# A two-layer flow block on one core: the low half of the grouped-query keys stored on 128 rows instead of 64

## The chip, the cores and the metric

The kernel runs on one core of a Trainium2 chip. It is one launch: inputs come from device memory, the result goes back to device memory, and what is measured is the device time of that launch in microseconds (us). Five engines work side by side, each through its own list of instructions: TensorE (PE, with its weight loads shown apart as PEld), VectorE (DVE), ScalarE (ACT), GpSimd (POOL), and SyncE (SP), which issues the transfers. Times are the median of three runs. One further execution was profiled, and it gives the rows below.

## The reference, cut to what matters

The model has two layers over 512 latent tokens and 256 context tokens, width 1024. Each layer mixes tokens in four groups (a convolution, a latent attention "MLA", a grouped-query attention "GQA", a retention) and ends in a feed-forward block. The change touches the scores of GQA alone: four query heads of width 64 share two key heads, and all 768 keys are seen by the latent queries.

```python
def grouped_attention(q, k, v):          # q: [b, kv, group, lq, 64]
    scale = dq ** -0.5
    def one_block(qblk):
        s = jnp.einsum('bkgqd,bksd->bkgqs', qblk, k) * scale
        p = jax.nn.softmax(s, axis=-1)
        return jnp.einsum('bkgqs,bksd->bkgqd', p, v)

yc_l = merge_heads(grouped_attention(gqa_q(q_l, gqa_q_g, pos),
                                     jnp.concatenate([gk_c, gk_l], axis=2),
                                     jnp.concatenate([gv_c, gv_l], axis=2)))
...
x = x + g1 * y_lat
x = x + g2 * sq_relu_mlp(modulate(x, sh2, sc2), mlp_w1[layer], mlp_w2[layer])
```

In layer 0 the context tokens are queries as well (over the 256 context keys); in layer 1 only the latents are.

## The kernel before, in words

**Numbers.** TensorE is fed with tiles of type F32R. So that little is lost, an fp32 operand x is kept as two such tiles, a high half (x copied to F32R) and a low half (x minus the high half). `split` writes both: a copy, then a subtraction. A product of two such operands is the sum of high times low, high times high and low times high, all summed in PSUM.

**GQA scores.** A head has width 64, half of TensorE's 128 rows. `gqa_prep` puts that to use. For each key head it transposes the keys into PSUM (64 rows by 512 latent or 256 context keys) and writes three things: `kd`, the high half, twice, on rows 0 to 63 and again on rows 64 to 127 (lines 1399 and 1400); and `kl`, the low half, on rows 0 to 63 (line 1401). For each unit (a query head and a pair of token tiles) it writes `qd`: the high half of the queries on rows 0 to 63, the low half on rows 64 to 127. The scores are then two passes (line 1089): pass 0 takes 64 rows of `qd` as stationary and `kl` as moving operand, which is high times low; pass 1 takes all 128 rows of `qd` and `kd`, which is high times high plus low times high. Each pass is one weight load and one matmul for 512 keys and one for 256 keys.

**Units.** A unit has two query tiles. For each there are the passes into one PSUM tile of 768 scores, a minimum over them on DVE, an exponential with its sum on ACT, a reciprocal on DVE, and a scaling on DVE, ACT or POOL (`scores`). `finish`, which is recorded after the next unit's scores, transposes the probabilities on TensorE, splits them, and multiplies them with the values. In layer 0 GQA has 12 units (4 heads by 3 pairs of tiles), of which the 4 on context tokens see only 256 keys; in layer 1 it has 8. So pass 0 is run 8·2·2 + 4·2·1 = 40 times in layer 0 and 8·2·2 = 32 times in layer 1, 72 times in all.

**Order.** The program is recorded first and then scheduled by a planner in the same file (`Plan`, lines 112 to 645), which holds an own cost for every instruction, walks a clock, and gives each engine its list of instructions. The list is fixed when the kernel runs. The planner's cost of a matmul goes by its columns and not by its rows. Some copies may go to DVE, ACT or POOL; the planner picks. All instructions are issued from line 645, so the profile's rows bear that line, and SBUF pages are all named `m`, PSUM banks `b` (one bank) or `pp` (two-bank tiles or halves of them), small columns `ty`.

Of the kernel before, what the change touches and what calls it, by code (L numbers as in the profile page):

```python
# [9 lines left out]
F32 = mybir.dt.float32  # L10
F32R = mybir.dt.float32r
AF = mybir.ActivationFunctionType
ALU = mybir.AluOpType
# [686 lines left out]
def block_kernel(ctx: ExitStack, tc: tile.TileContext, x, c, cx, c_ctx, w_mod, b_mod, w_in, w_out,  # L700
# [11 lines left out]
    V, S, G, T, D = plan.V, plan.S, plan.G, plan.T, plan.D  # L712
# [13 lines left out]
    def smt(shape, dt=F32, nm="sm"):  # L726
        return plan.tile(ph, "sm", shape, dt, nm)
# [13 lines left out]
    def psT(shape=(128, 512), nm="psT"):  # L741
        return plan.tile(ph, "t", shape, F32, nm, gang=True)
# [265 lines left out]
    def mixing(l, ht, yt, todo, late=None):  # L1008
# [9 lines left out]
        p = psT()  # L1018
# [8 lines left out]
        p = psT()  # L1027
# [38 lines left out]
        def tile_of(d, t):  # L1066
            for pr in PAIRS:
                if t in pr:
                    return d[pr][:, pr.index(t)]
# [317 lines left out]
        def gqa_prep(h, pr, whole):  # L1387
            def f():
                kv = h // 2
                if kv not in kgs:  # L1390
                    kds = {}
                    for a, ts in ((0, LAT), (512, CTX)):
                        p = psT()
                        n = 128 * len(ts)
                        kd, kl = kds[a] = [a3t([128, n], F32R, nm="kd") for _ in range(2)]
                        for i, t in enumerate(ts):
                            T.transpose(p[0:64, i * 128:(i + 1) * 128], tile_of(ug, t)[:, 256 + kv * 64:320 + kv * 64],
                                        ident)
                        VS.copy(out=kd[0:64], in_=p[0:64, 0:n])
                        VS.copy(out=kd[64:128], in_=p[0:64, 0:n])  # L1400
                        V.tensor_tensor(out=kl[0:64], in0=p[0:64, 0:n], in1=kd[0:64].bitcast(F32), op=ALU.subtract)
                    kgs[kv] = kds
                kds = kgs[kv]
                qd = smt([128, 256], F32R, nm="qd")
                p = psT()
                for i in range(2):
                    T.transpose(p[0:64, i * 128:(i + 1) * 128], ug[pr][:, i, h * 64:h * 64 + 64], ident)
                VS.copy(out=qd[0:64], in_=p[0:64, 0:256])
                V.tensor_tensor(out=qd[64:128], in0=p[0:64, 0:256], in1=qd[0:64].bitcast(F32), op=ALU.subtract)
                return (lambda i, n: qd[0:(64, 128)[n], i * 128:(i + 1) * 128],  # L1410
                        lambda n, a: kds[a][1][0:64] if n == 0 else kds[a][0],
                        (lambda t: tile_of(ug, t)[:, 384 + kv * 64:448 + kv * 64]) if whole else
                        (lambda t: tile_of(vg, t)[:, kv].rearrange("p a d -> p (a d)")))
            return f
# [487 lines left out]
```

## Time and profile before

| | |
|---|---|
| median of 3 runs | 1861.64 us (1861.56 to 1864.9) |
| the profiled execution | 1851.87 us |
| its span, first to last instruction | 1850.2 us |
| mean granted TensorE clock | 0.971 of full speed |
| PE busy | 1713.0 us, 93% of the span |
| DVE busy | 1356.5 us, 73% |
| ACT, POOL busy | 678.8 us (37%), 386.4 us (21%) |
| read from device memory | 161.14 MB, 88 GB/s over the span |

The first row of the table is what a change is measured by, the second is the execution that the trace shows. "Busy" is a share over the whole span, and the stages differ: the feed-forward blocks are long runs of matmuls, while in the two stretches with GQA scores (about 334 to 472 us in layer 0 and 1334 to 1426 us in layer 1) TensorE, DVE and ACT hand work to each other. The rows on those stretches stand further below. In the rows, `64*128` is a stationary operand of 64 rows and 128 columns, and the next figure, as 64x512, the moving operand.

### The profile page before, as it was taken

To read this page: it belongs to the slowest core of one execution; us is meant where nothing else is said; L and a number is where in the kernel's file an instruction comes from. 1 tells how busy PE (TensorE), PEld (TensorE's weight loads), DVE (VectorE), ACT (ScalarE), POOL (GpSimd) and SP (SyncE) were. 2 spreads that over 40 slices of the span, in tenths; PEclk is the share of its full clock that TensorE was granted. 3 is DMA by queue.
4 is the path that set the end of the run, shared out by engine and by line. 5 is a ranking of instruction groups with operands and counts; after the bars stand their busy time and mean duration, and the time that the engine had idled before them with its cause. 6 is when DMAs were issued, how large, how long until landed. Compare 5 with 4: busy or idle time off the path is not lost. (4 is left out here: it accounts for less than half of the span.)

```text
span 1850.2 us, 23212 instructions
## 1 busy us (share of the span) xinstructions
PE 1713.0 (93%) x8587; PEld 1393.5 (75%) x8587; DVE 1356.5 (73%) x2305; ACT 678.8 (37%) x1256; POOL 386.4 (21%) x355
## 2 busy tenths in 40 slices
PE   6995789989999999999999999959898989999998
PEld 4784668655788888888888889758766778888886
DVE  5889348877897788777775677974988776666665
ACT  5522028866434112112112126213987331122122
POOL 3328013541401000100100022120434521100001
PEclk9997899989999999999999999969999999999999
DMA  9220022443232334334331212110122523333331
GB/s 303 67 75 12 19 79 80 139 118 115 79 112 72 103 114 144 108 113 148 124 93 58 68 48 84 44 52 12 32 61 74 166 81 102 105 100 92 102 92 57
DMA packets 140641, 168.67 MB, mean 91 GB/s; under 512 B 7658, under 2 KB 93274, under 8 KB 140528
## 3 DMA queue, kind: packets, MB, share of 16 engines
q1 hardware_dynamic: 140528, 167.20, 29.4%
q8 instruction: 67, 1.10, 0.2%
q14 instruction: 46, 0.38, 0.1%
HBM read 161.14 MB, written 2.10 MB: 88 GB/s over the span
## 5 line engine op out<-in xcount | busy, mean ns | idle before, releaser
L645 PE MATMUL b<-m,m 128*128 128x512 f32 (+6 forms) x6400 | 1347.8, 368 | 43.3 <-DVE m L645 32.3
L645 PEld LDWEIGHTS b<-m,m 128*128 128x128 f32 (+2 forms) x6400 | 1107.2, 189 | 257.0 <-DVE m L645 30.4
L645 DVE TENSOR_TENSOR m<-m,m 128x1024 fp32r<-128x1024 f32 (+10 forms) x669 | 549.5, 840 | 135.0 <-PE b L645 81.2
L645 ACT CAST m<-m 128x1024 fp32r<-128x1024 f32 (+5 forms) x354 | 277.3, 804 | 661.5 <-PE b L645 470.0
L645 POOL TENSOR_TENSOR m<-m,m 128x1024 fp32r<-128x1024 f32 (+11 forms) x155 | 261.0, 1693 | 1106.2 <-ACT m L645 613.4
L645 DVE TENSOR_TENSOR m<-b,m 128x512 f32<-128x512 f32 (+12 forms) x337 | 203.7, 614 | 121.5 <-PE b L645 105.4
L645 PE MATMUL pp<-m,m 128*128 128x512 f32 (+9 forms) x904 | 227.1, 371 | 22.1 <-ACT m L645 10.9
L645 PEld LDWEIGHTS pp<-m,m 128*128 128x128 f32 (+3 forms) x904 | 153.0, 190 | 76.4 <-issue 24.2
L645 PE MATMUL b<-ident,m 128*128 128x128 f32 (+4 forms) x744 | 114.3, 279 | 32.3 <-DVE m L645 29.4
L645 ACT COPY m<-b 128x512 f32<-128x512 f32 (+6 forms) x177 | 82.0, 483 | 128.3 <-PE b L645 123.5
L645 PEld LDWEIGHTS b<-ident,m 128*128 128x128 f32 (+4 forms) x744 | 86.3, 141 | 53.9 <-DVE m L645 34.3
L645 DVE TENSOR_TENSOR m<-m 128x512 f32<-128x512 f32 (+2 forms) x107 | 67.4, 631 | 77.1 <-ACT m L645 76.4
L645 DVE CAST m<-m 128x512 fp32r<-128x512 f32 (+6 forms) x163 | 76.9, 474 | 57.6 <-DMA m<-in_w_mod_dram 31.3
L645 DVE SCALAR_TENSOR_TENSOR m<-m,sf,m 128x1024 f32<-128x1024 f32 x80 | 103.6, 1307 | 19.6 <-DMA m<-in_w_mod_dram 19.6
L645 ACT ACTIVATE m<-b 128x512 f32<-128x512 f32 (+1 forms) x117 | 61.8, 531 | 152.6 <-PE b L645 150.1
L645 DVE SCALAR_TENSOR_TENSOR m<-m,cvw,m 128x783 f32<-128x783 f32 (+1 forms) x120 | 100.8, 890 | 0.6
L645 DVE TENSOR_REDUCE ty<-pp 128x1 f32<-128x768 f32 (+1 forms) x67 | 61.9, 929 | 20.0 <-PE pp L645 19.5
L645 ACT ACTIVATE m<-pp,ty 128x768 f32<-128x768 f32 (+1 forms) x67 | 59.1, 883 | 14.2 <-DVE ty L645 6.1
L645 ACT ACTIVATE m<-m 128x1024 f32<-128x1024 f32 (+4 forms) x65 | 42.0, 649 | 51.3 <-DVE m L645 41.6
L645 POOL TENSOR_TENSOR ty<-ty,mhalf 128x1 f32<-128x1 f32 (+4 forms) x47 | 58.6, 1253 | 2.0
L645 DVE TENSOR_SCALAR m<-m,ty 128x512 f32<-128x512 f32 (+3 forms) x98 | 49.7, 542 | 8.8 <-POOL ty L645 8.1
L645 ACT CAST m<-b 128x512 fp32r<-128x512 f32 (+6 forms) x84 | 41.2, 500 | 38.6 <-PE b L645 37.6
(113 smaller groups left out, 629.5 us busy)
## 6 DMA issues: line engine op xcount, KB each, us to landing
m<-in_mlp_w_dram SPq DMA_DIRECT2D x128, 512.0 KB
m<-in_w_mod_dram SPq DMA_DIRECT2D x96, 512.0 KB
m<-in_w_in_dram SPq DMA_DIRECT2D x32, 512.0 KB
m<-in_w_out_dram SPq DMA_DIRECT2D x16, 512.0 KB
m<-in_x_dram SPq DMA_DIRECT2D x8, 512.0 KB
m<-in_dist_dram SPq DMA_DIRECT2D x16, 256.0 KB
m<-in_w_in_dram SPq DMA_DIRECT2D x8, 416.0 KB
m<-m SPq DMA_DIRECT2D x24, 96.0 KB
```

The costliest lines, as they stand in the source:

```text
L645: op.fn(*[f(a) for a in op.args], **{k: f(a) for k, a in op.kw.items()})
```

## The change

The low half of the keys is written a second time, to rows 64 to 127 of `kl`, by one more subtraction on DVE for each key head and each of the two key ranges: 8 instructions in all. Pass 0 then takes the whole of `qd` (128 rows) as its stationary operand and the whole of `kl` as the moving one. It so computes high times low plus low times low. The number of matmuls and weight loads stays what it was.

```diff
                         V.tensor_tensor(out=kl[0:64], in0=p[0:64, 0:n], in1=kd[0:64].bitcast(F32), op=ALU.subtract)
+                        V.tensor_tensor(out=kl[64:128], in0=p[0:64, 0:n], in1=kd[0:64].bitcast(F32), op=ALU.subtract)
                     kgs[kv] = kds
...
-                return (lambda i, n: qd[0:(64, 128)[n], i * 128:(i + 1) * 128],
-                        lambda n, a: kds[a][1][0:64] if n == 0 else kds[a][0],
+                return (lambda i, n: qd[:, i * 128:(i + 1) * 128],
+                        lambda n, a: kds[a][1 - n],
                         (lambda t: tile_of(ug, t)[:, 384 + kv * 64:448 + kv * 64]) if whole else
```

Since the planner sees eight more instructions, it gives other lists for the mixing stages of both layers. In the feed-forward blocks the rows stay the same but for the names of pages, apart from a few rows that follow a mixing stage.

On DVE, at the second key head of layer 0, the low half for the latent keys (tile `m_6987`, out of PSUM tile `pp_6699`) was one subtraction of 64x512 behind the two copies of the high half:

```order
L645 TENSOR_TENSOR m_6034<-b_3587,m_6034 64x256
L645 CAST m_5011<-pp_6699 64x512 x2
L645 TENSOR_TENSOR m_6987<-pp_6699,m_5011 64x512
L645 CAST m_6941<-b_3585 64x256 x2
L645 TENSOR_SCALAR kdt_914<-kdt_914 128x16
```

With the change, the same place has the tile under the name `m_7017`, from `pp_6957`, with the first of the two copies of the high half four rows further up:

```order
L645 CAST m_6034<-pp_6957 64x512
L645 TENSOR_REDUCE ty_3568<-pp_6981 128x1
L645 TENSOR_TENSOR m_3638<-b_3587,m_3638 64x256
L645 TENSOR_TENSOR m_6924<-pp_6956,m_6924 64x256
L645 CAST m_6034<-pp_6957 64x512
L645 TENSOR_TENSOR m_7017<-pp_6957,m_6034 64x512
L645 RECIPROCAL ty_3569<-ty_3575 128x1
L645 TENSOR_TENSOR m_7017<-pp_6957,m_6034 64x512
L645 TENSOR_REDUCE ty_3565<-pp_7025 128x1
```

The second subtraction has come in behind a reciprocal and ahead of the minimum (the reduction) of a unit, and other work of DVE now stands between the copies.

On PE, the first latent unit's scores (into `pp_6579`, from the page `m_6283` with the low half, `m_3841` with the high half, `m_5961` and `m_6034` for the context keys) stood as one block of four:

```order
L645 MATMUL b_3585<-m_6538,m_4425 128x256 x4
L645 MATMUL pp_6579<-m_6283,m_5961 128x512
L645 MATMUL pp_6579<-m_3841,m_5961 128x512
L645 MATMUL pp_6579<-m_5961 128x256
L645 MATMUL pp_6579<-m_6034,m_5961 128x256
L645 MATMUL b_3587<-m_6476,sc 2x512
```

Now (into `pp_6561`, the queries and the low half both in `m_6283`) they stand among the matmuls of an MLA unit's values, into `pp_6546`:

```order
L645 MATMUL b_3586<-m_6437,sc 4x512
L645 MATMUL pp_6561<-m_6283 128x512
L645 MATMUL pp_6546<-m_6527,m_4516 128x256 x3
L645 MATMUL pp_6546<-m_6531,m_4584 128x256
L645 MATMUL pp_6561<-m_3841,m_6283 128x512
L645 MATMUL pp_6546<-m_6531,m_4584 128x256 x3
L645 MATMUL pp_6561<-m_6283 128x256
L645 MATMUL pp_6561<-m_6034,m_6283 128x256
L645 MATMUL pp_6546<-m_6569,m_4425 128x256
```

The same four matmuls are there, and other matmuls have moved in between the two passes.

## Rows read from the trace of the kernel before

**Rows 1.** The page: busy time of each engine over the span (share, instructions).

```profile
PE 1713.0 (93%) x8587; PEld 1393.5 (75%) x8587; DVE 1356.5 (73%) x2305; ACT 678.8 (37%) x1256; POOL 386.4 (21%) x355
```

**Rows 2.** Windows: busy us (x instructions) per engine, granted clock, DMA; seven stretches.

```profile
core 0: us, PE busy (x) PEld busy (x) DVE busy (x) ACT busy (x) POOL busy (x), PEclk, DMA share, GB/s
290.00:334.00 44.00, 41.48 (x289) 34.50 (x288) 42.09 (x94) 39.77 (x85) 22.33 (x18) 1.00 0.31 94
334.00:472.00 138.00, 129.56 (x611) 79.24 (x609) 107.59 (x218) 99.36 (x217) 52.19 (x50) 0.94 0.41 125
1290.00:1334.00 44.00, 39.10 (x255) 32.17 (x253) 42.44 (x95) 42.48 (x90) 13.79 (x12) 1.00 0.09 29
1334.00:1426.00 92.00, 83.41 (x408) 54.88 (x406) 76.47 (x159) 74.72 (x157) 35.49 (x40) 1.00 0.19 56
362.00:369.00 7.00, 7.00 (x22) 4.28 (x22) 4.68 (x6) 4.01 (x7) 2.61 (x2) 0.51 0.46 145
386.00:396.00 10.00, 7.23 (x23) 5.29 (x24) 7.41 (x18) 4.29 (x10) 2.33 (x4) 0.50 0.40 101
1201.00:1232.00 31.00, 11.24 (x35) 8.97 (x36) 29.64 (x103) 5.06 (x7) 12.05 (x16) 0.51 0.09 26
```

**Rows 3.** Timeline of PE, 348.6 to 353.2: start us, us, tiles, form, count.

```profile
348.37 0.40 PE L645 MATMUL b<-m,m 128*128 128x256 f32 x2
348.70 0.92 PE L645 MATMUL pp<-m,m 64*128 64x512 f32 x2
...
351.78 0.92 PE L645 MATMUL pp<-m,m 64*128 64x512 f32 x2
352.63 0.38 PE L645 MATMUL pp<-m 64*128 64x256 f32 x1
352.94 0.38 PE L645 MATMUL pp<-m,m 128*128 128x256 f32 x1
353.17 0.40 PE L645 MATMUL b<-m,sc 128*4 128x512 f32 x1
```

**Rows 4.** Timeline of PEld in the same stretch: each weight load.

```profile
351.77 0.18 PEld L645 LDWEIGHTS pp<-m,m 64*128 64x128 f32 x1 [0.47 <-issue]
352.20 0.19 PEld L645 LDWEIGHTS pp<-m,m 128*128 128x128 f32 x1 [0.24 <-issue]
352.63 0.18 PEld L645 LDWEIGHTS pp<-m 64*128 64x128 f32 x1 [0.24 <-issue]
```

**Rows 5.** Timeline of PE in both feed-forward blocks: 128x512, 128x256 back to back.

```profile
1599.65 8.60 PE L645 MATMUL b<-m,m 128*128 128x512 f32 x37
...
842.82 2.79 PE L645 MATMUL b<-m,m 128*128 128x256 f32 x22
```

**Rows 6.** Groups of PE by form: 64-row stationaries (two of five).

```profile
L645 PE MATMUL pp<-m,m 64*128 64x512 f32 x26 | 13.1, 505 | 2.6 <-DVE m L645 1.6 <-ACT m L645 0.8
L645 PE MATMUL pp<-m,m 64*128 64x256 f32 x33 | 13.0, 393 | 0.0
```

**Rows 7.** Waits of DVE, 334:472 and 1334:1426: us, times, longest us.

```profile
DVE ty L645 <- PE pp L645: 9.6, 12, 2.4
...
DVE ty L645 <- PE pp L645: 7.7, 7, 1.9
```

**Rows 8.** Timeline of DVE, then PE, at the second key head of layer 0.

```profile
385.63 0.68 DVE L645 TENSOR_TENSOR m<-pp,m 64x512 fp32r<-64x512 f32 x1
...
386.46 2.00 PE L645 MATMUL pp<-m,m 64*128 64x512 f32 x3 [1.61 <-DVE m L645]
```

**Rows 9.** Groups of DVE by form: 64-row subtractions out of PSUM.

```profile
L645 DVE TENSOR_TENSOR m<-b,m 64x256 fp32r<-64x256 f32 x14 | 5.8, 417 | 0.4
...
L645 DVE TENSOR_TENSOR m<-b,m 64x512 fp32r<-64x512 f32 x3 | 2.0, 671 | 0.0
```

**Rows 10.** Timeline of PE, from 1219 us, ahead of a fall of the clock.

```profile
1219.06 1.11 PE L645 MATMUL pp<-ident,m 128*128 128x128 f32 x4 [5.45 <-ACT m L645]
1228.10 18.13 PE L645 MATMUL b<-m,m 128*128 128x384 f32 x81 [7.92 <-DVE m L645]
```

## The prediction, made before the changed kernel was run

> **What bounds the kernel now.** I read the page first, then windows over the two stretches with grouped-query scores, then the order of time on PE inside one of them. The page says that PE is busy for 93% of the span and DVE for 73% [rows 1], so a PE microsecond is the likeliest to count. The windows say where that is less sure [rows 2]. In layer 0 the score stretch, 334 to 472 us, has PE at 129.56 of 138 us, DVE at 107.59 and ACT at 99.36: PE leads. In layer 1, 1334 to 1426 us, it is PE 83.41, DVE 76.47, ACT 74.72 of 92: three engines nearly level. Who waits for whom agrees: DVE's minimum stands still for the score matmuls for 9.6 us in the first stretch and 7.7 us in the second [rows 7], so the scores come late, and DVE would take them earlier.
>
> In the order of time the score matmuls are dearer than their sizes. Two passes over 512 and then 256 keys begin at 351.78 us, and the matmul behind them begins at 353.17: 1.39 us for four matmuls [rows 3]. In the feed-forward blocks a 128x512 matmul follows another after (8.60 - 0.40)/36 = 0.228 us, the last one's own length of 0.40 taken off; 22 matmuls of 128x256 last 2.79 us and two of them 0.40, so 20 more steps are 2.39 us and one is 0.120 [rows 5, 3]. By these steps the four should take 2(0.228 + 0.120) = 0.70 us. The weight loads show where the rest goes: between 64-row and 128-row stationaries PEld stands idle for 0.24 us with nothing named but issue, and a load begins only as its own matmul does (351.77 against 351.78) [rows 3, 4]. So PE seems to empty itself each time the row count of the stationary changes, before the 64-row pass and again behind it.
>
> **The change, part by part.** *Pass 0 on 128 rows.* Within the four matmuls 1.39 - 0.70 = 0.69 us are lost. One more loss lies ahead of them: the two 128x256 matmuls that stand before a 64-row pass take 0.33 us from 348.37 to 348.70, where two steps are 0.24 [rows 3]: 0.09 us. That is 0.78 us for two 64-row passes, 0.39 us each. There are 72 of them, 40 in layer 0 and 32 in layer 1 (two of the forms, 59 of the 72, are shown) [rows 6]. With all stationaries on 128 rows the change of rows is gone, and with it 40 x 0.39 = 15.6 us of PE in layer 0 and 32 x 0.39 = 12.5 us in layer 1, 28.1 us together. The matmuls and weight loads stay as many, and none has more columns. A few visits gain less, where PE has yet another kind of stationary next to them, and a few lie at half clock, in 362 to 369 and 386 to 396 us [rows 2], and gain more; I leave both out.
>
> What of this reaches the end? Layer 0: without the 15.6 us the stretch would be 122.4 us long, and DVE would need 107.6 us plus its new work (1.1 us, below), 89% of it. DVE has been at 42.09 of 44 us, 96%, in the stretch just before [rows 2], so it isn't yet the bound; but the chains through the exponential are not shorter than they were and PE has less work to cover them. PE now has 8.4 us without work there; I let that grow by 3 and take 12.6 us. Layer 1: without the 12.5 us the stretch would be 79.5 us, in which DVE needs 77.6. At the 96% that it has shown, its floor is 80.8 us, so at most 11.2 us can be gained, and only if ACT (74.7) and DVE are both kept full. DVE is now at 83% there. At 92%, between the two, the stretch is 84.4 us long: a gain of 7.5 us, rounded, which I take. Both stretches: 20.1 us. Late next are the exponentials on ACT and the splits and minima on DVE.
>
> *Eight more subtractions.* One of 64x512 takes 0.67 us and one of 64x256 0.42 us [rows 9], so each of the four key heads (two a layer) costs DVE 1.1 us. The first key head of each layer is prepared just ahead of the score stretches, where DVE is at 42.09 and 42.44 of 44 us [rows 2]: nothing covers them there, 2.2 us. The minima, splits and copies that are queued behind them go later by as much, and PE's transposes and matmuls wait for those. For the second head of layer 0, PE's first 64-row matmul at 386.46 us had waited 1.61 us for DVE, whose 64x512 subtraction had begun at 385.63 [rows 8]: a second one, which the order puts behind a reciprocal, adds 0.7 us to that wait, and what stands behind that matmul in PE's list waits with it. For the second head of layer 1 I count nothing more than the 1.1 us in DVE's need above. Together 2.9 us; bounds are 0, if the order has room for all of it, and 8 subtractions with nothing beside them, 4 x 1.09 = 4.4 us.
>
> *Other lists.* The planner has moved many rows in both mixing stages. No row of before prices that. The nearest that bounds it are PE's idle times in the two stretches, 8.4 and 8.6 us [rows 2]: at best half of them could go, and as likely they could grow by half. I take 0, with -8 and +8 us as ends.
>
> *The sum.* 20.1 - 2.9 = 17.2 us. The profiled execution, 1851.87 us, would become 1834.7. The median of the runs stands 0.53% above that execution, so I carry the ratio: 1861.64 x 1834.7 / 1851.87 = 1844.4, said as **1844.5 us**.
>
> **A rule that speaks against it.** Weight loads of 128 rows do run beside matmuls of 128 rows: 37 matmuls of 128x512 follow each other at 0.228 us, though a load takes 0.19 [rows 4, 5]. The Trainium skill (TensorE: Matmul & The Clock Gate, section "The mechanism" under packing small matmuls) says that a weight load overlaps with a running matmul only if the two use different groups of rows. By that rule every full-height load would stand in the open, a step would be near 0.23 + 0.19 = 0.42 us whatever the rows, and the change would save nothing. The trace disagrees for full-height pairs, so I follow the rows; what is left of the thought is the third rival.
>
> **The rivals.** (1) *All of it arrives, and the clock too.* The 28.1 us of PE come through, and the falls to half clock in 362 to 369 and 386 to 396 us (17 us, granted 0.50 [rows 2]) go away because PE is less often empty: up to 8.5 us more. For it: DVE's waits for scores, 17.3 us in all [rows 7]. Against it: DVE's floor in layer 1. Time: 1861.6 less 25 to 36.6, so 1825 to 1837.
>
> (2) *DVE takes PE's place at once.* Layer 1 gives nothing, since DVE and ACT were level with PE; layer 0 gives half, 7.8 us; the subtractions cost 2.9. Time: 1861.6 - 4.9 = 1856.7, within 1852 to 1858. For it: 42 of 44 us of DVE just ahead of both stretches.
>
> (3) *The rows are not the cause.* The 0.24 us belongs to the change of tile or of PSUM bank and stays, so that the change does not do what it says: only the subtractions are left, 1861.6 + 0 to 4.4. Against it: the gap stands between the two passes over the same 512 keys too, which write the same scores (352.20 us), and in the feed-forward blocks matmuls that add into one bank follow at the ordinary step [rows 4, 5].
>
> (4) *Slower, by the clock.* PE does less in the same time, and where it already waited long its clock was at half: in 1201 to 1232 us, with waits of 5.45 and 7.92 us, PE was busy for 11.24 of 31 us and the granted clock was 0.51 [rows 2, 10]. If the waits of layer 1's score stretch grow so that the clock falls there, its 70.9 us of remaining PE work (83.4 - 12.5) would take up to 70.9 us more; half of the stretch at half clock costs some 35 us. Less the 17.2 us gained this is 1861.6 + 18 = 1880; it turns slower from about 17 us of added PE time on. Against it: that stretch ran at a granted clock of 1.00 with PE idle for 8.6 of its 92 us [rows 2].
>
> **How the numbers follow.** Forecast 0.56 (its own range 1837 to 1852), rival 1 0.14, rival 2 0.15, rival 3 0.07, rival 4 0.04, and 0.04 for the new lists alone undoing the gain (1858 to 1866). About 0.2%, 3.7 us, is what a measurement can tell from no change. Faster takes the forecast, rivals 1 and 2, less a little of the latter: 0.84. Within 0.2% takes part of rival 3 and of the lists: 0.08. Slower takes the rest: 0.08. The range runs from the middle of rival 1 to the end of rival 2: 1830 to 1859.
>
> **What would show it.** No weight load of 64 rows among the scores; four score matmuls followed by others within 0.75 us in place of 1.39; eight more subtractions on DVE; the score stretch of layer 0 near 126 us long and that of layer 1 near 85; DVE's waits for scores down to half. The feed-forward blocks should last as long as before. Wrong would be steps of 0.43 us between 128-row passes that stay, or a stretch that stays as long with DVE above 95%.

## The result and the profile after

| | before | after |
|---|---|---|
| median of 4 runs each | 1863.27 us (1861.56 to 1866.37) | 1847.38 us (1843.48 to 1847.7) |
| ratio, 95% interval | | 0.9899 [0.9876, 0.9921] |
| the profiled execution, span | 1851.87, 1850.2 us | 1847.59, 1845.9 us |
| granted clock | 0.971 | 0.958 |

The changed kernel is 1.0% faster: 15.9 us by the medians, 18.8 us by the ratio. A later measurement gave 0.9898 [0.9858, 0.9937] (after_again, below). The two profiled executions lie only 4.3 us apart, which needs a word before any row is compared. In the long middle part, from the first feed-forward matmuls of layer 0 to the first scores of layer 1, the work is the same in both but for two of the added subtractions (1.1 us of DVE), and yet it took 734.0 us in the first trace of before and 745.5 in that of after. Windows over that part, first before, then a later trace of before, then after; the columns are stretch, length, busy us (count) of PE, PEld, DVE, ACT and POOL, granted clock, DMA share and GB/s:

```profile
core 0: us, PE busy (x) PEld busy (x) DVE busy (x) ACT busy (x) POOL busy (x), PEclk, DMA share, GB/s
600.00:1334.00 734.00, 699.36 (x3615) 598.43 (x3614) 534.21 (x879) 200.37 (x362) 85.08 (x85) 0.98 0.28 85
```

```profile
598.80:1339.00 740.20, 703.98 (x3615) 602.77 (x3614) 534.06 (x879) 200.54 (x362) 84.66 (x85) 0.97 0.28 84
```

```profile
587.90:1333.40 745.50, 707.77 (x3616) 605.74 (x3615) 534.00 (x880) 201.73 (x362) 87.78 (x88) 0.96 0.28 84
```

The clock column differs: 0.98, 0.97, 0.96. The first trace of before happened to run longer at full clock than the others, so a comparison of whole profiled spans hides a good part of the gain. From here on I compare the two parts that hold the scores and nearly all that differs in the lists: from the 1451st to the 2707th matmul of PE (layer 0, first scores to feed-forward) and from the 6321st to the 7151st (layer 1). In before the first key head of each layer is prepared ahead of them. Each sum of the two repeats within 1 us: 450.6 and 451.1 us in the two traces of before, 431.4 and 431.3 in the two of after. By that the change gave 19 us, and both layers have a share: 267.3 to 251.8 and 183.3 to 179.6 us. A single part is less sure than that: in lists_b (below), whose list on PE is before's throughout layer 0, the first one took 263.2 us.

Windows of after, the two parts and, in them, the stretches with scores (the answer to [rows 2]):

```profile
336.10:587.90 251.80, 243.29 (x1258) 181.29 (x1257) 210.08 (x374) 154.18 (x304) 91.86 (x85) 0.96 0.38 115
1333.40:1513.00 179.60, 157.83 (x832) 126.94 (x831) 149.88 (x257) 115.48 (x219) 69.41 (x58) 0.93 0.31 97
336.10:466.70 130.60, 122.31 (x621) 78.89 (x620) 111.23 (x228) 102.87 (x216) 60.56 (x55) 0.92 0.43 135
1333.40:1427.70 94.30, 77.52 (x407) 57.98 (x407) 82.83 (x166) 77.23 (x160) 37.55 (x36) 0.88 0.17 51
```

By the same counts of matmuls the score stretch of layer 0 was 139.3 us (138 in [rows 2]) and is 130.6; that of layer 1 was 93.2 us (92 in [rows 2]) and is 94.3. PE is busy for only 77.52 of these 94.3 us, at a granted clock of 0.88. On the page PE's busy time has gone from 1713.0 us [rows 1] to

```profile
PE 1706.8 (92%) x8587; PEld 1403.2 (76%) x8587; DVE 1355.0 (73%) x2309; ACT 684.3 (37%) x1257; POOL 394.6 (21%) x358
```

although more of the span ran at half clock (a granted clock of 0.5). No matmul with 64 rows is left among the scores. The order of time on PE in layer 1, start and duration in us, with the two passes over 512 keys, one matmul of another unit, and the two passes over 256 keys:

```profile
1347.05 0.62 PE L645 MATMUL pp<-m,m 128*128 128x512 f32 x2
1347.50 0.28 PE L645 MATMUL b<-m,m 128*128 128x256 f32 x1
1347.62 0.40 PE L645 MATMUL pp<-m,m 128*128 128x256 f32 x2
1347.86 0.27 PE L645 MATMUL b<-ident,m 128*128 128x128 f32 x1
```

From 1347.05 to 1347.86 these five take 0.81 us, just the 2 x 0.228 + 3 x 0.120 = 0.82 of the ordinary steps; four of them without the other took 1.39 us before [rows 3]. DVE's waits for scores, 9.6 and 7.7 us before [rows 7], are in the same two stretches of after:

```profile
DVE ty L645 <- PE pp L645: 3.2, 3, 2.2
```

```profile
DVE ty L645 <- PE pp L645: 3.4, 3, 2.1
```

The trace has eight 64x512 subtractions out of PSUM (6 and 2) where before had four.

### The profile page after: what moved, and what is told of

Its sections match the earlier page's. It is cut to its first block, busy times and chain, and to the rows that moved or that the text cites. A ratio compares the mean times of both kernels' runs of the same rounds, so it can differ in the third digit from the quotient of the medians.

```text
span 1845.9 us, 23213 instructions
## 1 busy us (share of the span) xinstructions
PE 1706.8 (92%) x8587; PEld 1403.2 (76%) x8587; DVE 1355.0 (73%) x2309; ACT 684.3 (37%) x1257; POOL 394.6 (21%) x358
## 5 line engine op out<-in xcount | busy, mean ns | idle before, releaser
L645 PE MATMUL b<-m,m 128*128 128x512 f32 (+5 forms) x6452 | 1366.8, 370 | 49.6 <-DVE m L645 40.7
L645 DVE TENSOR_TENSOR m<-m,m 128x512 fp32r<-128x512 f32 (+8 forms) x665 | 548.9, 844 | 138.0 <-PE b L645 79.9
L645 ACT CAST m<-m 128x1024 fp32r<-128x1024 f32 (+6 forms) x354 | 278.8, 808 | 666.2 <-PE b L645 462.8
L645 PE MATMUL pp<-m,m 128*128 128x512 f32 (+6 forms) x848 | 206.0, 369 | 18.9 <-DVE m L645 9.7
L645 PEld LDWEIGHTS pp<-m,m 128*128 128x128 f32 (+2 forms) x848 | 148.1, 197 | 56.0 <-ACT m L645 15.8
L645 ACT COPY m<-b 128x512 f32<-128x512 f32 (+7 forms) x176 | 82.8, 491 | 126.6 <-PE b L645 120.4
L645 DVE TENSOR_TENSOR m<-m 128x256 f32<-128x256 f32 (+1 forms) x104 | 63.4, 611 | 82.9 <-ACT m L645 82.4
L645 DVE CAST m<-m 128x512 fp32r<-128x512 f32 (+4 forms) x163 | 77.8, 481 | 56.3 <-PE pp L645 31.7
L645 PE MATMUL pp<-ident,m 128*128 128x128 f32 (+3 forms) x252 | 41.6, 287 | 13.4 <-ACT m L645 7.5
L645 POOL TENSOR_SCALAR ty<-ty 128x2 f32<-128x2 f32 (+4 forms) x43 | 16.3, 380 | 166.3 <-ACT m L645 107.3
```

Of the source, the lines that this page charges most:

```text
L645: op.fn(*[f(a) for a in op.args], **{k: f(a) for k, a in op.kw.items()})
```

## The experiments

The edits are shown condensed. The theory, A: PE empties itself at each change between a 64-row and a 128-row stationary, and the change takes these away. The first rival, B: the planner's other lists bring the gain. Rows and lists can be parted, since the lists are fixed in the program: a kernel can be planned in one way and issue wider or narrower operands at the same places. Four kernels make a square: before's lists with 64 rows (subs_only) and with 128 (same_order), the new lists with 64 rows (new_order_64) and with 128 (the change itself).

**same_order.** The planner sees the kernel before. At issue, pass 0 takes the wide operands, and each subtraction of the low half is followed at once by its sibling.

```diff
+    V.tensor_tensor(out=kl[0:64], ...)          # recorded as before; at issue, behind it:
+    plan.twin[at_] = dict(out=kl[64:128])
...
+    if n == 0 and self.npass == 2:              # recorded with 64 rows; at issue:
+        plan.as_[at_] = dict(lhsT=qd[:, i * 128:(i + 1) * 128], rhs=kds[a][1])
```

> Before's lists on every engine, row for row, with pass 0 on 128 rows and the eight added subtractions each right behind its sibling (two pass-0 matmuls are put off until the low half of the queries is written). Theory A (PE empties itself at each change between 64-row and 128-row stationaries, and that is what the change takes away): no step of 0.31 or 0.43 us is left among the scores, 28 us of PE go, and the time falls by 12 to 22 us, ratio 0.988 to 0.994. Rival B (the gain of the changed kernel comes from the planner's other lists): within 3 us of before, or slower by up to 4 us for the subtractions.

**new_order_64.** The planner sees the changed kernel; at issue pass 0 takes 64 rows.

```diff
+    if n == 0 and self.npass == 2:              # recorded with 128 rows; at issue:
+        plan.as_[at_] = dict(lhsT=qd[0:64, i * 128:(i + 1) * 128], rhs=kds[a][1][0:64])
```

> The changed kernel's lists, row for row, with all subtractions, but pass 0 reads 64 rows of both operands as before (the low half on rows 64 to 127 is written and not read). Theory A: the steps of 0.31 and 0.43 us are back, 28 us of PE with them, and the time is that of before, 1856 to 1872 us, ratio 0.997 to 1.005. Rival B (the lists): the time is that of the changed kernel, ratio 0.99.

**subs_only.** Before, with the siblings of the subtractions alone.

```diff
+    plan.twin[at_] = dict(out=kl[64:128])
```

> Before's lists and before's 64-row pass 0, with only the eight subtractions added, each right behind its sibling. The prediction's term: 2.9 us slower, between 0 and 4.4 (ratio 1.0000 to 1.0024). If the lists of DVE have room there, 0.

Measured, with the two parts from the traces:

| | ratio to before [95%] | layer 0, layer 1, sum (us) | PE busy at half clock in them (us) |
|---|---|---|---|
| before, two traces | 1 | 267.3 + 183.3 = 450.6; 266.1 + 185.0 = 451.1 | 21.6; 20.9 |
| subs_only: old lists, 64 rows | 1.0021 [0.9999, 1.0044] | 271.0 + 185.0 = 456.0 | 33.1 |
| same_order: old lists, 128 rows | 0.9936 [0.9909, 0.9962] | 259.8 + 182.1 = 441.9 | 34.0 |
| new_order_64: new lists, 64 rows | 0.9961 [0.9935, 0.9986] | 257.5 + 186.0 = 443.5 | 31.9 |
| after: new lists, 128 rows | 0.9899 [0.9876, 0.9921] | 251.8 + 179.6 = 431.4 | 37.9 |

Both A and B hold. The rows give 456.0 - 441.9 = 14.1 us under the old lists and 12.1 under the new; the lists give 12.5 us with 64 rows and 10.5 with 128. The last column, from the clock records of the traces, is the clock's part in this. In same_order a step of 128x512 is 0.43 us at half clock and 0.23 at full, so an estimate takes half of that column off each sum: the rows then give some 15 us under either lists, and the lists some 12 with either rows. The two parts of subs_only are 5 us longer than those of before, but by the same estimate nothing of that is left (439.4 us against 439.8 and 440.6), so these 5 us are not shown to be the subtractions' own; whether the subtractions brought the lower clock about is not shown either.

The timed ratios give 0.85 and 0.62% for the rows, each from two intervals that do not overlap. For the lists they give 0.60 and 0.37%; the intervals behind the second overlap. For the subtractions they give 0.21%, 3.9 us, with an interval that just reaches zero. So theory A's expectation for new_order_64 was met by its time, 1857.28 us, but not by its ratio (0.997 to 1.005) nor by its reason: the 64-row losses were back, and better lists made up for a part of them.

What the rows give can be read where before's block of four matmuls stood [rows 3, 4]. PE and then PEld in same_order, at the same place in the list:

```profile
353.37 0.62 PE L649 MATMUL pp<-m,m 128*128 128x512 f32 x2
353.83 0.28 PE L649 MATMUL pp<-m 128*128 128x256 f32 x1
353.95 0.28 PE L649 MATMUL pp<-m,m 128*128 128x256 f32 x1
354.07 1.08 PE L649 MATMUL b<-m,sc 128*4 128x512 f32 x4
```

```profile
353.14 0.42 PEld L649 LDWEIGHTS pp<-m,m 128*128 128x128 f32 x2
353.61 0.19 PEld L649 LDWEIGHTS pp<-m 128*128 128x128 f32 x1
353.83 0.19 PEld L649 LDWEIGHTS pp<-m,m 128*128 128x128 f32 x1
```

From 353.37 to 354.07 it is 0.70 us, which is what the ordinary steps make, in place of 1.39; and the weight loads begin ahead of their matmuls (353.61 for 353.83, where it was 352.63 for 352.63).

Theory A expected no step of 0.31 or 0.43 us to be left among the scores. Some are left. Of 28 passes over 512 keys with the low half that ran at full clock in same_order, 12 have a step of 0.23 to 0.24 us and 16 one of 0.31 to 0.43. Seven of the 16 stand beside a stationary of 64 columns (`128*64`), as this one does, between two of them (same_order, window 1384 to 1392 us):

```profile
1387.54 3.66 PE L649 MATMUL b<-m,m 128*64 128x512 f32 x14
1391.13 0.50 PE L649 MATMUL pp<-m 128*128 128x512 f32 x1
1391.56 0.64 PE L649 MATMUL b<-m,m 128*64 128x512 f32 x1
```

Its step is 0.43 us, that of a 64-row pass. Three more of the 16 came right after a wait of PE; for the other six no cause was found.

What the rows are worth to a stretch, by windows over the scores of layers 0 and 1, subs_only and then same_order:

```profile
336.90:476.80 139.90, 131.18 (x620) 80.57 (x618) 109.29 (x222) 99.81 (x217) 52.63 (x51) 0.94 0.41 125
1352.20:1447.10 94.90, 84.61 (x409) 56.15 (x407) 78.92 (x162) 74.80 (x157) 36.75 (x41) 0.98 0.18 54
```

```profile
335.80:466.00 130.20, 119.40 (x620) 78.43 (x620) 107.40 (x222) 98.81 (x216) 51.62 (x51) 0.93 0.45 134
1341.60:1431.90 90.30, 77.25 (x408) 56.23 (x406) 79.91 (x161) 74.55 (x157) 37.04 (x41) 0.96 0.19 57
```

PE's busy time falls by 11.8 and 7.4 us, the stretches by 9.7 and 4.6: PE's idle time grows from 8.7 to 10.8 us and from 10.3 to 13.1. DVE's share of layer 1 goes from 83 to 88%.

What the subtractions cost shows at the second key head of layer 0, where PE had waited 1.61 us [rows 8]. DVE, then PE, in subs_only:

```profile
388.28 0.68 DVE L648 TENSOR_TENSOR m<-pp,m 64x512 fp32r<-64x512 f32 x1
388.98 0.68 DVE L650 TENSOR_TENSOR m<-pp,m 64x512 fp32r<-64x512 f32 x1
```

```profile
389.81 1.70 PE L648 MATMUL pp<-m,m 64*128 64x512 f32 x3 [2.31 <-DVE m L650]
```

The sibling takes 0.68 us and PE's wait is now 2.31 us. That is one place; what all eight cost the kernel stays open, as said above.

What the lists give lies mostly behind the scores of layer 0. PE's waits there in subs_only (idle before, and who ended it, in brackets), and windows from the end of the scores to the feed-forward matmuls for subs_only, new_order_64 and after:

```profile
484.34 0.99 PE L648 MATMUL b<-m,m 128*64 128x256 f32 x4 [1.92 <-DVE m L648]
...
560.10 0.66 PE L648 MATMUL b<-ident,m 128*128 128x128 f32 x4 [1.54 <-DVE m L648]
...
574.28 0.30 PE L648 MATMUL b<-ident,m 128*128 128x128 f32 x1 [1.61 <-DVE m L648]
```

```profile
476.80:607.90 131.10, 125.06 (x638) 105.03 (x638) 106.46 (x154) 50.77 (x86) 28.84 (x31) 0.97 0.29 86
```

```profile
468.10:589.40 121.30, 120.98 (x640) 102.40 (x639) 98.39 (x146) 51.28 (x88) 31.31 (x31) 1.00 0.31 93
```

```profile
466.70:587.90 121.20, 120.98 (x640) 102.40 (x639) 98.85 (x147) 51.31 (x89) 31.30 (x31) 1.00 0.31 93
```

131.1 us became 121.3 and 121.2; in the two traces of before, with the old lists, the same matmuls took 128.0 and 130.9, so the lists give 7 to 10 us there. PE was idle for 6.0 us of the first and for 0.3 and 0.2 of the others; DVE has 8 us less to do there, and over the whole part of layer 0 7 us less, while POOL has 11 and ACT 4 us more: the planner has moved work that more than one of them can do. And the clock stayed at 1.00 where it was 0.97. Windows over the whole part of layer 0, subs_only and new_order_64:

```profile
336.90:607.90 271.00, 256.24 (x1257) 185.59 (x1256) 215.75 (x376) 150.57 (x303) 81.47 (x81) 0.96 0.35 106
```

```profile
331.90:589.40 257.50, 252.16 (x1258) 181.64 (x1257) 208.84 (x374) 154.31 (x304) 92.31 (x85) 0.97 0.37 112
```

In layer 1 the new lists lose in the scores what they gain behind them: from subs_only to new_order_64 the score stretch went from 94.9 to 100.5 us, and what follows it from 90.1 to 85.5. The score stretch of layer 1 in new_order_64:

```profile
1333.20:1433.70 100.50, 85.86 (x409) 59.03 (x407) 83.10 (x169) 77.63 (x161) 38.16 (x36) 0.90 0.16 48
```

**grouped_64.** Before's lists but for one move: in the 32 scores of latent tiles, the second pass over 512 keys is put behind the first pass over 256.

```diff
+    if self.npass == 2 and nk == 768:
+        if (a, n) == (0, 1): put_off = at_
+        elif (a, n) == (512, 0): plan.need[put_off] = at_      # issue put_off right behind this one
```

> Before's lists but for one move: for each latent query tile (32 of them) the 128-row pass over the first 512 keys comes behind the 64-row pass over the next 256, so that two 64-row passes stand side by side. Still 72 matmuls of 64 rows, but 40 visits to 64 rows instead of 72. Theory A (each change of rows costs): 32 x 0.39 = 12.5 us of PE go, the time falls by 5 to 11 us, ratio 0.994 to 0.997, and the second of two 64-row matmuls follows the first at the ordinary step of 0.23 us. Rival C (a 64-row matmul is slow by itself): no change, within 2 us, and each 64-row step stays at 0.31 or 0.43 us.

0.9955 [0.9928, 0.9982], 445.0 us in the two parts: 8.4 us faster by the ratio and 5.6 to 6.1 by the traces of before. That agrees with A; for C, still 72 matmuls of 64 rows, nothing should have moved. PE's busy time in the two score stretches is 7 to 10 us below that of the two traces of before, where 12.5 were expected. In one more point the expectation was wrong:

```profile
350.18 0.39 PE L649 MATMUL b<-m,sc 128*2 128x512 f32 x1
350.50 0.50 PE L649 MATMUL pp<-m,m 64*128 64x512 f32 x1
350.83 0.28 PE L649 MATMUL pp<-m 64*128 64x256 f32 x1
351.04 0.61 PE L649 MATMUL pp<-m,m 128*128 128x512 f32 x2
351.50 0.85 PE L649 MATMUL b<-m,sc 128*4 128x512 f32 x3
```

The second 64-row matmul comes 0.33 us after the first and not 0.23. The four steps show how a change of rows is paid: the matmul ahead of it takes 0.32 where 0.23 is ordinary (350.18 to 350.50), the first one behind it 0.33 (to 350.83); then again the last of 64 rows 0.21 for 0.12 (to 351.04) and the pair behind it 0.46 for 0.35. So at this place each change costs 0.09 us on the matmul ahead and 0.10 to 0.11 on the one behind, 0.2 us in all, and a visit to 64 rows has two of them.

**rows_96.** same_order with 96 rows in pass 0.

```diff
-        plan.as_[at_] = dict(lhsT=qd[:, i * 128:(i + 1) * 128], rhs=kds[a][1])
+        plan.as_[at_] = dict(lhsT=qd[0:96, i * 128:(i + 1) * 128], rhs=kds[a][1][0:96])
```

> The kernel same_order (before's lists, eight subtractions beside their siblings), but pass 0 takes 96 rows of both operands instead of 128, so that the row counts still alternate, 96 and 128. It leaves out low times low for half of the head's columns. Theory A1 (what empties PE is a stationary that fits in half of the rows beside one that does not): the steps are the ordinary ones, 0.23 and 0.12 us, and the time is that of same_order, ratio to before 0.991 to 0.996. Rival A2 (any change of the row count does it): steps of 0.31 and 0.43 us, and the time is that of subs_only, 1.000 to 1.004.

0.9932 [0.9906, 0.9958], 258.6 + 183.2 = 441.8 us: same_order to within 0.1 us. PE at the same place:

```profile
350.48 0.63 PE L649 MATMUL pp<-m,m 96*128 96x512 f32 x2
350.95 0.28 PE L649 MATMUL pp<-m 96*128 96x256 f32 x1
351.07 0.28 PE L649 MATMUL pp<-m,m 128*128 128x256 f32 x1
351.19 1.09 PE L649 MATMUL b<-m,sc 128*4 128x512 f32 x4
```

0.71 us for the four. Rival A2 falls: 96 rows beside 128 cost nothing, 64 beside 128 do.

**no_pass0.** What holds layer 1 once the steps are ordinary? Here pass 0 is left out.

```diff
+        if op.idx in self.skip: continue        # pass 0
...
+        plan.as_[at_] = dict(start=True)        # pass 1 begins the sum
```

> same_order without pass 0 (the products with the low half of the keys are left out, in both layers): 72 matmuls and weight loads fewer, 12.1 us of PE at the ordinary steps, 6.5 in layer 0 and 5.6 in layer 1. Theory D (in layer 1 the chain through DVE and ACT holds the stretch once PE's steps are ordinary, in layer 0 PE still does): the score stretch of layer 0 (128.9 us in same_order) gets 4 to 6 us shorter, that of layer 1 (90.3 us) under 2 us, with more idle PE. Rival E (PE still holds both): both get shorter by their whole 6.5 and 5.6 us, 12 us in all below same_order.

0.9886 [0.9852, 0.9920], below same_order by 0.5%, 9 us, by the ratios and by 5.4 us by the medians (1846.32 against 1851.73, on two chips on which before's medians are 1.7 us apart), with intervals that overlap. Windows over the scores, cut at the same instructions of DVE, same_order and then no_pass0:

```profile
337.60:466.40 128.80, 118.00 (x610) 77.31 (x609) 105.80 (x221) 98.19 (x215) 51.77 (x50) 0.93 0.45 133
1342.10:1431.90 89.80, 76.75 (x404) 55.73 (x402) 79.41 (x161) 74.05 (x156) 36.72 (x40) 0.96 0.19 57
```

```profile
335.90:459.70 123.80, 111.59 (x573) 70.06 (x573) 105.99 (x221) 97.93 (x216) 51.80 (x50) 0.94 0.46 138
1330.90:1419.80 88.90, 75.20 (x373) 54.28 (x372) 80.43 (x162) 73.41 (x156) 40.08 (x39) 0.90 0.19 58
```

Layer 0 gets 5.0 us shorter for 6.4 us less of PE, layer 1 only 0.9 us, both as theory D had it. The second number is not clean: no_pass0's clock was 0.90 there against 0.96. PE's idle time rose from 13.1 to 13.7 us, so the rest of layer 1's saving went into slower matmuls, not into waits. That layer 1 is held by DVE and ACT is likely by their shares (90 and 83% of the stretch) but is not shown by this run.

**Other lists.** Is a gain from lists owed to the added subtractions? lists_b and lists_b2 are before with other lists, got by a change that computes the same; lists_a is the changed kernel treated as lists_b2.

```diff
-    VS.copy(out=kd[0:64], in_=p[0:64, 0:n])              # lists_b: these two in the other order
-    VS.copy(out=kd[64:128], in_=p[0:64, 0:n])
+    V.tensor_copy(out=kd[0:64], in_=p[0:64, 0:n])        # lists_b2, lists_a
+    S.copy(out=kd[64:128], in_=p[0:64, 0:n])
```

> Before, unchanged in what it computes and with 64-row passes, but the two copies of the high half of the keys are recorded in the other order, which gives other lists in the mixing stages (379 rows of PE differ). Theory G (before's lists are one draw among many, and the waits behind the scores of layer 0 at 461, 480, 554 and 568 us, some 6 us, belong to that draw): the time differs from before by up to 8 us either way, and the stretch from the first scores of layer 0 to the first feed-forward matmuls (267 us in before) by as much. Rival H (it is the added subtractions that lead the planner to better lists): within 3 us of before.

> As lists_b, with one copy of the high half of the keys tied to DVE and the other to ACT instead of the planner's choice (1409 rows of PE differ from before). Theory G: up to 8 us either way. Rival H: within 3 us of before.

> The changed kernel (128-row passes, eight subtractions) with one copy of the high half of the keys tied to DVE and the other to ACT (1269 rows of PE differ from the changed kernel). Against lists_b2 it shows the change under a third pair of lists. Theory A with G: 5 to 22 us faster than lists_b2, since the rows give 9 to 14 and the lists add -8 to +8; 1840 to 1862 us. If the change's gain were mostly the lists' luck, it would be within 5 us of lists_b2.

lists_b: 1.0001 [0.9980, 1.0021], 263.2 + 185.6 = 448.8 us. lists_b2: 0.9959 [0.9941, 0.9976], 259.5 + 183.5 = 443.0. lists_a: 0.9893 [0.9867, 0.9919], 248.2 + 182.9 = 431.1. lists_b tests less than its expectation says: on PE its list differs from before's in layer 1 alone. Layer 0's part, with before's list on PE, was:

```profile
335.40:598.70 263.30, 249.37 (x1258) 180.98 (x1257) 214.86 (x374) 150.93 (x305) 83.96 (x81) 0.99 0.37 110
```

The granted clock was 0.99 there, and 6.8 us ran at half clock; in the two traces of before it was 17.1 and 13.7. So the 4 us by which this part is shorter are hardly a gain of lists (on DVE six rows have changed places). But lists_b2 beats before's lists by 7.6 us without any change of the scores, and H falls; under this third pair the change is worth 11.9 us in the parts, 0.66% by the ratios, within the 5 to 22 that were named.

**mixed, after_again and before_again.** mixed has the new lists in layer 0 and the old ones in layer 1 (it records the changed kernel in layer 0 and same_order in layer 1).

> Layer 0 with the changed kernel's lists, layer 1 with before's lists, pass 0 on 128 rows in both. The traces so far: the new lists save some 7 us behind the scores of layer 0 and lose 4 us in the scores of layer 1 against same_order, but save 4 to 5 behind those. Theory F (each layer's lists act for themselves): the score stretch of layer 1 near 90 us instead of the 94 of the changed kernel, the rest as there, 1843 to 1851 us, ratio 0.987 to 0.991, so equal to the changed kernel or up to 4 us faster. Rival: the clock's falls decide, and it is slower than the changed kernel by 3 us or more.

> The changed kernel once more, beside the others on one chip. Ratio 0.988 to 0.992; the split into lists and rows adds up if it is near 0.9961 (new_order_64) less 0.0085 (same_order against subs_only), 0.9876.

> Before once more, for its trace. The first trace had 106 us at half clock, those of the other kernels 130 to 150. If that is chance, this one has 120 to 150 us at half clock and a time of 1860 to 1870 us, with the score stretches as long as in the first (138 and 93 us).

mixed: 0.9872 [0.9837, 0.9908], 249.0 + 180.8 = 429.8 us, against 0.9898 and 431.3 for after_again beside it. The score stretch of layer 1 was 89.7 us as F has it, but what lies behind took that back, and the intervals overlap: mixed is not shown to beat the change, nor is lists_a. before_again ran in 1858.91 us, with 451.1 us in the two parts; its score stretches were 135.3 and 94.1 us, the first shorter than the 138 expected: 6.8 us of it ran at half clock, and 17.1 us in the first trace. The whole execution had 127 us at half clock, within the 120 to 150 expected (109 in the first trace), and its time lay 1 us below the 1860 to 1870. after_again's ratio is in its range; the 0.9876 at which the split into lists and rows would add up lies within its interval, and no more can be said.

## Why the prediction came out right, point by point

**The bound and the mechanism: right.** PE led, the loss lay at the changes between 64 and 128 rows, and the change took all 72 visits away. In same_order loads of 128 rows begin 0.22 us ahead of their matmuls, among matmuls of 128 rows (353.61 and 353.83). The rule that spoke against the change, from the Trainium skill (TensorE: Matmul & The Clock Gate, section "The mechanism"), would have them wait; the trace disagrees. The prediction took only half of that section of the Trainium skill: it also lets a load go ahead of running matmuls when it goes into the background weight buffer. With that half the trace agrees. Another rule of the Trainium skill (TensorEngine Tiling (Array Packing), section "Key Properties") says that a change of the tiling mode drains TensorE; that page of the Trainium skill lists, under "Available Configurations", arrays of 64 rows and of 64 columns as modes and none of 96 rows. The trace agrees: 0.2 us at each change of rows in grouped_64, nothing in rows_96, and 0.43 us for a 128-row pass between two stationaries of 64 columns.

**Step "pass 0 on 128 rows": right kind, too large.** The 0.39 us of a visit were read at a place where four matmuls stand by themselves, and there they were right (1.39 to 0.70 us). Over all 72 visits 28.1 us were forecast for PE; under the same lists PE's busy time fell by 11.8 + 7.4 = 19.2 us. Some of the 9 us that are missing can be found. In before 12 of the 72 matmuls of 64 rows have a stationary of 64 columns next to them; there the change of rows goes and a change of columns stays. The prediction had left such neighbours out as a few that gain less. In all, the 16 slow steps that are left in same_order are 1.7 us above the ordinary 0.228. Another 1.7 us is the clock: in layer 1's stretch PE was busy at half clock for 6.8 us in same_order and 3.4 in subs_only. The rest is open.

**What reaches the end: forecast 12.6 + 7.5 = 20.1 us, measured 9.7 + 4.6 = 14.3** in the score stretches under the old lists. Of what PE did save, three quarters arrived, near the share that I had taken (72%); the term was too large because its input was. Layer 1 was rightly the poorer one. In the changed kernel itself its stretch did not get shorter at all: 94.3 us, not near 85, with DVE at 88% of it and not above 95. That is the lists: with the new ones and 64 rows it was 100.5 us, so the rows gave 6 us there and the lists took as much. PE waited 16.8 us in it, at a granted clock of 0.88, which looks like rival 4; but with 64 rows the same lists already had PE waiting for 14.6 us at 0.90, so most of it did not come from PE's saved work.

**The subtractions: 2.9 us forecast; 3.9 by the ratio, [-0.2, 8.2], so not settled.** The one place that was worked out came to the tenth, 1.61 to 2.31 us of waiting. The 2.2 us for the first key heads lie ahead of the two parts, and no run tells them apart there: layer 0's part begins at 333.0 to 336.9 us in the kernels with before's lists and the siblings (subs_only, same_order, rows_96) and at 331.9 to 335.4 without them (before, before_again, grouped_64, lists_b). The 5 us in the two parts go with the clock.

**"Other lists: 0, with -8 and +8 as ends": the step that failed.** The new lists gave 10.5 us with 128 rows and 12.5 with 64. I had bounded them by PE's idle time within the score stretches, but the lists changed what comes behind as well: there 6 us of PE's waits for DVE went, the clock stayed up, and 7 to 10 us were gained that no term of mine named.

**The sum, -17.2 us, is near the measured -15.9 to -18.8 because two misses cancel, and that is luck:** the rows gave 14.3 us in the score stretches and not 20.1, the lists 7 to 13 us and not 0; what the subtractions took is not settled. Of the rivals, (1), (2) and (4) did not happen; (3) is refuted by the square and by rows_96; the new lists, which I had listed only as a danger of 0.04, were a gain.

## What to carry to other kernels

Before saving rows of a stationary operand, look at what stands beside it: here a 64-row matmul among 128-row ones cost up to 0.4 us more than a full one, and the 72 of them some 12 to 16 us. The eight subtractions of 0.4 to 0.7 us on DVE that took them away could not be told from no cost. Stationaries of 64 columns deserve the same look. If narrow stationaries are needed, put them side by side. And where a planner writes the order, part the change from its lists (plan one, issue the other) before crediting either; here the two were worth 12 to 16 and 7 to 13 us. And before a part of a trace is compared, see how much of it ran at half clock.

## What the runs showed of the hardware that was not expected

- A stationary of 96 rows beside one of 128 costs nothing (rows_96: 0.71 us for four matmuls, 0.70 with 128 rows); one of 64 does (1.39 us). Each change between 64 and 128 rows costs about 0.2 us where it was read (grouped_64), half on the matmul ahead of it and half on the one behind.
- Behind a stationary of 64 columns there is a loss of that kind too: there a 128x512 matmul with a stationary of 128 columns has a median step of 0.34 us where 0.23 is ordinary, and one of 128x256 one of 0.20 where 0.12 is (same_order, 8 and 11 of them).
- With the same lists and the same work, the middle part took 734.0 us in one execution and 740.2 in another of the same kernel, with the granted clock at 0.98 and 0.97: for this kernel one profiled span is a poor measure of a change of 1%.
